# Turning the raw input once: norms applied behind four projections instead of before them, in a two-block transformer kernel

## The chip, the cores and the metric

One core of one Trainium2 chip runs the whole program. The metric is the device time of one execution in microseconds, as the median of several runs. The engines are TensorE (PE, with its weight loads PEld), VectorE (DVE), ScalarE (ACT), GpSimd (POOL) and SyncE (SP, which here issues most of the transfers).

## The reference

Two blocks over 512 tokens of 1024 features, with 16 meta tokens in front (528 tokens in all). Only the start of the first block is touched by the change: the root-mean-square norm and the projections that use it. `w_in` is 1024 x 7168.

```python
def _rms(x, w, eps=1e-6):
    xf = x.astype(jnp.float32)
    y = xf * lax.rsqrt(jnp.mean(xf * xf, axis=-1, keepdims=True) + eps)
    return (y * w.astype(jnp.float32)).astype(x.dtype)
...
        n = _rms(h, norm_mix_w[l])
        z = n @ w_in[l]
        q, k, v, glu, g_att, g_conv = jnp.split(z, splits, axis=-1)
...
        o = _diff_attention(q, k, v, lam, cid)
        y_att = (_rms(o, subln_w[l]) * (1.0 - lambda_init)).reshape(b, lp, ATT_V).astype(h.dtype)
        u = glu[..., :CONV_CH] * jax.nn.sigmoid(glu[..., CONV_CH:])
        u = _causal_dwconv(u, conv_dw_w[l], conv_dw_b[l])
        u = jax.nn.silu(_layernorm(u, conv_ln_w[l], conv_ln_b[l]))
        y_conv = u @ w_conv_out[l]
        m = jax.nn.sigmoid(g_att) * y_att + jax.nn.sigmoid(g_conv) * y_conv
        h = h + m @ w_out[l]
```

The norm's inverse root is one number per token, so a projection of the input times the norm's weight, multiplied per token afterwards, is the same projection. After this come a feed-forward with a short convolution, a second block with three mixers, and its feed-forward.

## The kernel before

Activations lie by feature: 128 features on the partitions, tokens in the free direction, so a projection of 128 output columns is eight k tiles (`step`), each with three products: every fp32 operand is split into a high and a low part of type fp32r (h + l is the value), and high x high, high x low and low x high are added in PSUM. The 528 tokens go as two column segments, so a step is six matmuls of 256 to 264 columns. A weight chunk of 1024 x 128 is loaded by SP into one of three `raw` tiles, ACT makes its high part `wh`, DVE its low part `wl` (`weights`).

The program is written by a planner: `Build` keeps an estimate of PE's time and of DVE's and ACT's, and emits the main stream of projections while side tasks (generators that yield the time until their next step) are put between them; each engine then runs its instructions in the order of emission. All vector and scalar calls are recorded at line 158, all products at line 314, all transposes at line 320. PSUM has two tiles `mm` for the main stream and two tiles `at` for side tasks (`at_get`, `at_put`).

`load_x` loads the tokens as five row tiles `xt` (four of 128, one of 16). `prepare` squares and sums each tile on ACT, takes inverse roots in two groups, scales the rows on DVE into `xs`, and `parts` turns `xs` by 128 x 128 transposes on PE (five for each of eight feature tiles), multiplies by the norm's weight `wmix` and splits the result into the eight operands `xn`, which all projections of the block use. The unscaled input is needed by feature as well, for the residual `res`: feature tiles 0 to 3 are turned while the input loads (16 transposes into the `mm` tiles), the last 16 tokens of these and the feature tiles 4 to 7 by the task `raw`, which runs beside the first projections.

`block1_mix` runs the projections in the order of `units1`: first `glu(0)`, the pair of a convolution input's gate and value halves, k tile by k tile as the operands come, then query, key and value of head 0, the next pair, and so on. ACT evacuates the gate half with a tanh (`e_b`), DVE combines it with the value half (`e_a`); then 33 convolution steps on DVE run in the background (`conv_ops`). Query and key are evacuated by ACT (`e_q`, `e_k`).

## Time and profile before

| | |
|---|---|
| time of the kernel before | 1598.53 us, median of 3 runs (1594.26 to 1602.46) |
| span of the profiled execution | 1592.8 us; the page gives no other time for it |
| PE busy | 1573.0 us, 99% |
| DVE, ACT busy | 1116.7 us, 651.6 us |
| DMA | 134.17 MB, mean 84 GB/s |

The span runs from the first to the last instruction of the profiled execution, and the runs' times are of the whole execution, so the median is compared with the span with some us around it. Lines are those of the kernel before; names are the program's tiles without their numbers: `act` is the pool that holds nearly all activations, `xv` the sums of squares, `rsy` and `rsa` the inverse roots, `u` the convolution's input, `par` the per-channel parameters, `lams` and `lamd` the lambda of the attention.

### The profile page before, as it was taken

Reading aid. Unit: us, or ns where it says so; the run is one execution under the profiler, and the core shown is the slowest. Engines: PE = TensorE matmul, PEld = TensorE weight load, DVE = VectorE, ACT = ScalarE, POOL = GpSimd, SP = SyncE. Lnnn points to the kernel's source line nnn. Section 1 sums busy time; section 2 is a strip of 40 time slices with the busy share of each in tenths; the row PEclk is TensorE's granted clock in tenths of the full one; section 3 lists DMA queues with packets and bytes.
Section 4 is the critical chain, followed back from the end, with each engine's and each line's share of the span. In section 5 each row is a group of like instructions: output and inputs, shape, how many; then the busy total and the mean of one; then the engine's idle time right before and its main releaser. Section 6 shows DMA issues by size and latency. Waiting matters only on the chain.

```text
span 1592.8 us, 25470 instructions
## 1 busy us (share of the span) xinstructions
PE 1573.0 (99%) x10347; PEld 1402.3 (88%) x10349; DVE 1116.7 (70%) x2083; ACT 651.6 (41%) x1166; POOL 26.4 (2%) x85
## 2 busy tenths in 40 slices
PE   7999999999999999999999999999999999999998
PEld 6999999999999999999988878787799888888886
DVE  4989898987766567676753457899868877776224
ACT  5343434445453344344432222634466544444112
POOL 3000000000000000000000000000000000000000
PEclk9999999999999999999999999999999999999999
DMA  4312222212213233333323332232044133332221
GB/s 143 94 57 76 67 80 66 67 55 67 67 54 107 80 93 94 93 94 91 88 86 95 94 93 79 79 94 65 3 133 133 41 99 98 94 93 98 101 93 66
DMA packets 233004, 134.17 MB, mean 84 GB/s; under 512 B 6925, under 2 KB 228240, under 8 KB 232888
## 3 DMA queue, kind: packets, MB, share of 16 engines
q1 hardware_dynamic: 231448, 130.35, 27.9%
q8 instruction: 81, 1.33, 0.3%
q0 software_dynamic: 1136, 1.15, 0.2%
q10 hardware_dynamic: 304, 1.05, 0.2%
q14 instruction: 35, 0.29, 0.1%
HBM read 130.44 MB, written 2.10 MB: 83 GB/s over the span
## 4 chain that ended last, share of the span: by engine, by line
PE 97%; DVE 1%; ACT 1%; DMA 0%; issue 0%; DVEq 0%; ACTq 0%; POOLq 0%
PE mm L314 70%; PE at L314 25%; PE at L320 3%; ACT act L158 0%; DVE act L158 0%; DMA act<-in_x_dram 0%; DVE yy L158 0%; ACT ys L158 0%; DVE yc L158 0%; DVE smx L158 0%; DVE wl L158 0%; DVE fx L158 0%; DVE res L158 0%; DVEq L2194 0%; DVE srl L158 0%
## 5 line engine op out<-in xcount | busy, mean ns | idle before, releaser
L314 PE MATMUL mm<-act,wh 128*128 128x256 f32 (+3 forms) x4720 | 908.1, 306 | 1.2 <-ACT act L158 0.5
L314 PEld LDWEIGHTS mm<-act,wh 128*128 128x128 f32 (+1 forms) x4720 | 692.5, 189 | 51.8 <-issue 9.4
L314 PE MATMUL mm<-act,wl 128*128 128x256 f32 (+4 forms) x2360 | 563.0, 303 | 0.0
L158 DVE TENSOR_TENSOR wl<-raw,wh 128x1024 fp32r<-128x1024 f32 (+2 forms) x235 | 284.4, 1211 | 172.3 <-ACT wh L158 169.8
L158 ACT ACTIVATE wh<-raw 128x1024 fp32r<-128x1024 f32 (+2 forms) x235 | 245.8, 1048 | 377.2 <-PE mm L314 195.6
L314 PEld LDWEIGHTS mm<-act,wl 128*128 128x128 f32 (+1 forms) x2360 | 383.1, 189 | 18.1
L158 DVE SCALAR_TENSOR_TENSOR act<-u,par,act 128x514 f32<-128x514 f32 x232 | 160.4, 747 | 0.0
L314 PE MATMUL at<-act,wh 128*128 128x512 f32 x416 | 130.2, 394 | 0.0
L314 PEld LDWEIGHTS at<-act,wh 128*128 128x128 f32 x416 | 78.0, 188 | 18.3
L314 PE MATMUL at<-wh,act 128*128 128x512 f32 x264 | 85.9, 395 | 0.0
L314 PE MATMUL at<-act,act 128*128 128x256 f32 (+8 forms) x468 | 83.8, 328 | 0.0
L314 PE MATMUL mm<-wh,act 128*128 128x256 f32 (+1 forms) x344 | 83.7, 318 | 0.0
L314 PE MATMUL at<-act,wl 128*128 128x512 f32 x208 | 82.0, 394 | 0.0
L158 DVE TENSOR_TENSOR act<-act,act 128x514 f32<-128x514 f32 (+4 forms) x122 | 69.9, 590 | 6.4 <-ACT act L158 5.8
L158 ACT ACTIVATE act<-mm 128x528 f32<-128x528 f32 (+2 forms) x64 | 35.2, 550 | 94.4 <-PE mm L314 91.8
L314 PEld LDWEIGHTS at<-act,act 128*128 128x128 f32 (+1 forms) x468 | 60.7, 189 | 10.1 <-issue 4.0
L158 DVE SCALAR_TENSOR_TENSOR ft<-fx,par,ft 128x512 f32<-128x512 f32 x88 | 65.8, 749 | 1.6
L158 ACT ACTIVATE act<-at 128x128 f32<-128x128 f32 (+4 forms) x88 | 34.7, 413 | 78.5 <-PE at L314 61.9
L158 DVE TENSOR_TENSOR fx<-mm,rB 128x514 f32<-128x514 f32 x44 | 30.5, 694 | 50.2 <-PE mm L314 50.0
L314 PEld LDWEIGHTS mm<-wh,act 128*128 128x128 f32 x344 | 57.8, 189 | 7.1 <-issue 3.2
L158 DVE SCALAR_TENSOR_TENSOR gy<-gx,par,gy 128x512 f32<-128x512 f32 x84 | 62.6, 749 | 1.5
L314 PEld LDWEIGHTS at<-wh,act 128*128 128x128 f32 x264 | 49.6, 188 | 11.4
(288 smaller groups left out, 1470.6 us busy)
## 6 DMA issues: line engine op xcount, KB each, us to landing
raw<-in_w_in_dram SPq DMA_DIRECT2D x82, 512.0 KB, 3.6
raw<-in_w_up_dram SPq DMA_DIRECT2D x44, 512.0 KB, 3.6
raw<-in_ffn_up_dram SPq DMA_DIRECT2D x44, 512.0 KB, 3.7
raw<-in_ffn_down_dram SPq DMA_DIRECT2D x22, 512.0 KB, 3.2
raw<-in_w_out_dram SPq DMA_DIRECT2D x20, 512.0 KB, 3.8
raw<-in_w_down_dram SPq DMA_DIRECT2D x16, 512.0 KB, 3.6
raw<-in_w_conv_out_dram SPq DMA_DIRECT2D x8, 512.0 KB, 3.7
raw<-in_w_down_dram SPq DMA_DIRECT2D x8, 384.0 KB, 3.3
```

What stands on the lines that cost most here:

```text
L158: return f(*a, **k)
L314: self.nc.tensor.matmul(out, lhsT, rhs, start=start, stop=stop)
L320: self.nc.tensor.transpose(out, src, self.ident[p0 : p0 + k, p0 : p0 + k])
```

## The change

The input is turned once, as it is: feature tiles 0 and 1 row tile by row tile while the input loads, into the two `at` tiles, the others in `parts`. From each turned tile come, in this order, its split times the norm's weight (`xr`), and the copy for the residual (`res`, by ACT). The pair `glu(0)` and query and key of head 0 multiply by `xr`, that is by the input without the inverse norms; these are applied when the results leave PSUM, by DVE with `r0`, the inverse norms of all tokens on every partition, which `stats` makes from the squares (now behind the first splits on ACT), a Newton step, five diagonal tiles and five products with ones. The normed operands `xn` of all other projections are made by `norm`, by feature: DVE multiplies `res` by the weight column and `r0`, and the result is split by ACT and DVE. The scaling by token, the second turning and the task `raw` are gone. The diff below leaves out changes of comments; lines that only say "..." stand for what is left out.

```diff
@@ load_x @@
     def load_x(self):
         nc, io, V, S = self.nc, self.io, self.V, self.S
         x, meta = io["x"][0], io["meta_tokens"]
         self.res = [self.resp.tile([P, NT], F32, name=f"res{j}", tag="res") for j in range(KD)]
-        self.xn = [None] * KD
+        self.xn, self.xr = [None] * KD, [None] * KD
         rows = [P, P, P, P, NMETA]
         xt = [self.flat(D) for _ in range(5)]
-        xs = [self.flat(D) for _ in range(5)]
+        junk = self.flat(D)
         v = self.sm(5, "xv")
         V.memset(v, 1.0)
-        at = (1, 2, 3, 4, 0)
@@ -620,108 +620,103 @@
             else:
                 s = t * P - NMETA
                 q.dma_start(xt[t][: rows[t], :], x[s : s + rows[t], :])
-            self.loaded(xt[t], 5.0 + 1.55 * t)
+            self.loaded(xt[t], 6.5 + 1.2 * t)
...
         wmix = self.const.tile([P, 8], F32, name="wmix")
-
-        def turn(src, pt, j):
-            for t in range(5):
-                w = rows[t]
-                self.tr(pt[:, t * P : t * P + w], src[t][:w, j * P : (j + 1) * P])
-
-        def scale(ts, r, g):
-            c = slice(512 * g, 512 * g + 512)
-            for i, t in enumerate(ts):
-                V.tensor_scalar(xs[t][: rows[t], c], xt[t][: rows[t], c], r[: rows[t], i : i + 1], None, op0=MUL)
-
-        def inverse(lo, n):
-            vb = v[:, lo : lo + n]
-            yield self.due(vb)
-            V.tensor_scalar(vb, vb, 1.0 / D, 1e-6, op0=MUL, op1=ADD)
-            return (yield from self.rsqrt_act(vb, n))
-
-        raws = [self.mm_ps(), self.mm_ps()]
-        rawv = lambda j: raws[j // 2][:, (j % 2) * 512 : (j % 2) * 512 + 512]
+        self.r0 = None
+        rB0 = self.slot()[:, 0, :]
+        def turn(t, pt, j):
+            w = rows[t]
+            self.tr(pt[:, t * P : t * P + w], xt[t][:w, j * P : (j + 1) * P])
 
         def square(t):
-            S.activation(xs[t][: rows[t]], xt[t][: rows[t]], AF.Square, accum_out=v[: rows[t], at[t] : at[t] + 1])
+            S.activation(junk[: rows[t]], xt[t][: rows[t]], AF.Square, accum_out=v[: rows[t], t : t + 1])
 
         def prepare():
             S.activation(self.sm(1, "yw"), v[:, 0:1], AF.Sqrt)
-            self.tr(raws[1][:, 0:8], w8[0:8])
-            yield self.due(raws[1])
-            V.tensor_copy(wmix, raws[1][:, 0:8])
-            square(4)
+            i, pt = yield from self.at_get()
+            self.tr(pt[:, 0:8], w8[0:8])
+            yield self.due(pt)
+            V.tensor_copy(wmix, pt[:, 0:8])
+            self.at_put(i)
+            ats = []
+            for _ in range(2):
+                ats.append((yield from self.at_get()))
+            self.wp_max = 1
             for t in range(4):
                 yield self.due(xt[t])
-                square(t)
-                for j in range(4):
-                    self.tr(rawv(j)[:, t * P : (t + 1) * P], xt[t][:, j * P : (j + 1) * P])
+                for j in range(2):
+                    turn(t, ats[j][1], j)
                 if t == 0:
-                    r = yield from inverse(0, 2)
-                    for g in range(2):
-                        scale((4, 0), r, g)
-            r = yield from inverse(2, 3)
-            scale((1, 2, 3), r, 0)
-            self.wp_max = 1
+                    for j in range(2):
+                        turn(4, ats[j][1], j)
+                    square(4)
+                    square(0)
             for p in range(2):
-                self.start(parts(p))
-            yield self.due(raws[0])
-            for j in range(2):
-                S.activation(self.res[j][:, 0:512], rawv(j), AF.Copy)
-            yield self.due(xs[3][:, 0:512])
-            yield 4.0
-            scale((1, 2, 3), r, 1)
-            for j in range(2, 4):
-                S.activation(self.res[j][:, 0:512], rawv(j), AF.Copy)
-
-        def parts(p):
+                self.start(parts(p, *ats[p]))
+            self.start(stats(), 2.0)
+        def parts(p, i, pt):
             for j in range(p, KD, 2):
-                i, pt = yield from self.at_get()
-                yield self.due(*[xs[t][: rows[t], j * P : (j + 1) * P] for t in range(5)])
-                turn(xs, pt, j)
+                if j != p:
+                    i, pt = yield from self.at_get()
+                    for t in range(5):
+                        turn(t, pt, j)
                 yield self.due(pt)
                 n = self.slot(F32R)
                 self.split_scaled(n, pt[:, :NT], wmix[:, j : j + 1], NT)
-                self.xn[j] = n
+                S.activation(self.res[j], pt[:, :NT], AF.Copy)
+                self.xr[j] = n
                 if j == 1:
                     self.wp_max = 3
-                yield self.due(n)
+                yield self.due(n, self.res[j])
                 self.at_put(i)
 
-        def raw():
...
+        def stats():
+            for t in (1, 2, 3):
+                square(t)
+                yield 1.5
+            yield self.due(v)
+            V.tensor_scalar(v, v, 1.0 / D, 1e-6, op0=MUL, op1=ADD)
+            r = yield from self.rsqrt_act(v, 5)
+            yield from self.bcast_cols(r, rows, rB0, True)
+            yield self.due(rB0)
+            self.r0 = rB0
+            tmp = self.slot()
+            for p in range(2):
+                self.start(norm(p, tmp[:, p, :]))
+        def norm(p, t):
+            for j in range(p, KD, 2):
+                while self.xr[j] is None:
+                    yield 0.2
+                yield self.due(self.res[j])
+                V.scalar_tensor_tensor(t, self.res[j], wmix[:, j : j + 1], rB0, op0=MUL, op1=MUL)
+                yield self.due(t)
+                n = self.slot(F32R)
+                self.split_sb(n, t, NT)
+                self.xn[j] = n
+                yield 0.5
 
         self.feed = [0.0, self.weights()]
         self.start(prepare())
-        self.until(lambda: self.xn[0] is not None)
-        return raw
-
-    def one(self, segs, acts, evac):
+        self.until(lambda: self.xr[0] is not None)
+    def one(self, segs, acts, evac, have=None):
         pt = self.mm_ps()
         lo = segs[0][0]
         n = sum(s[1] for s in segs)
-        self.units([[(pt[:, o : o + m], m, c) for o, m, c in segs]], acts, evac=lambda u: evac(pt[:, lo : lo + n]))
+        self.units([[(pt[:, o : o + m], m, c) for o, m, c in segs]], acts, have=have,
+                   evac=lambda u: evac(pt[:, lo : lo + n]))
@@ block1_mix @@
-            self.start(raw(), 4.0)
             self.start(params(), 14.0)
...
@@ -1080,7 +1074,12 @@
             def glu(s):
                 def e_b(p):
                     hold["tb"] = self.slot()
-                    S.activation(hold["tb"][:, 0, :NT], p, AF.Tanh, scale=0.5)
+                    tb = hold["tb"][:, 0, :NT]
+                    if s == 0:
+                        self.until(lambda: self.r0 is not None)
+                        V.tensor_tensor(tb, p, self.r0, op=MUL)
+                        p = tb
+                    S.activation(tb, p, AF.Tanh, scale=0.5)
 
                 def e_a(p):
                     while len(self.bg) > CK + 2:
@@ -1088,6 +1087,8 @@
                     u = tp.tile([P, CK - 1 + NT], F32, name=self.nm("u"), tag="u")
                     nc.gpsimd.memset(u[:, : CK - 1], 0.0)
                     V.scalar_tensor_tensor(u[:, CK - 1 :], hold["tb"][:, 0, :NT], 1.0, p, op0=ADD, op1=MUL)
+                    if s == 0:
+                        V.tensor_tensor(u[:, CK - 1 :], u[:, CK - 1 :], self.r0, op=MUL)
                     if s % 2 == 0:
                         cv[s // 2] = self.slot()
                     self.until(lambda: "params" in state)
@@ -1101,9 +1102,9 @@
                             if 0 <= kk < 8:
                                 if kk == 0:
                                     ws.append(self.w_take())
-                                self.until(lambda: self.xn[kk] is not None)
+                                self.until(lambda: self.xr[kk] is not None)
                                 self.step([(pts[u][:, o : o + m], m, c) for o, m, c in SEG_ALL], ws[u],
-                                          self.xn[kk], kk, kk == 0, kk == 7)
+                                          self.xr[kk], kk, kk == 0, kk == 7)
                     self.wp_out -= 2
                     e_b(pts[0][:, 248:776])
                     e_a(pts[1][:, 248:776])
@@ -1118,10 +1119,16 @@
                     if h % 2 == 0:
                         ya[h // 2] = self.slot()
                     hold["qk"] = self.slot()
-                    S.activation(hold["qk"][:, 0, :NQ], p, AF.Copy)
+                    if h == 0:
+                        V.tensor_tensor(hold["qk"][:, 0, :NQ], p, self.r0[:, Q0:], op=MUL)
+                    else:
+                        S.activation(hold["qk"][:, 0, :NQ], p, AF.Copy)
 
                 def e_k(p):
-                    S.activation(hold["qk"][:, 1, :], p, AF.Copy)
+                    if h == 0:
+                        V.tensor_tensor(hold["qk"][:, 1, :], p, self.r0, op=MUL)
+                    else:
+                        S.activation(hold["qk"][:, 1, :], p, AF.Copy)
 
                 def e_v(p):
                     hold["vs"] = self.slot()
@@ -1131,7 +1138,9 @@
                     S.activation(hold["vs"][:, 1, :NQ], p, AF.Tanh, scale=0.5)
                     atts.append(self.attention(tp, h, hold["qk"], hold["vs"], (sx, v16, th16, w8, yav(h), state)))
 
-                self.one(SEG_ALL if i in (1, 2) else SEG_Q, self.xn, (e_q, e_k, e_v, e_g)[i])
+                acts = self.xr if h == 0 and i < 2 else self.xn
+                self.one(SEG_ALL if i in (1, 2) else SEG_Q, acts, (e_q, e_k, e_v, e_g)[i],
+                         have=lambda k: acts[k] is not None)
@@ tile_hybrid_kernel @@
-    raw = b.load_x()
-    b.block1_mix(raw)
+    b.load_x()
+    b.block1_mix()
```

## Rows read from the trace of the kernel before

**Rows 1.** The page's first part: each engine's busy time, its share of the span and its instructions.

```profile
PE 1573.0 (99%) x10347; PEld 1402.3 (88%) x10349; DVE 1116.7 (70%) x2083; ACT 651.6 (41%) x1166; POOL 26.4 (2%) x85
```

**Rows 2.** Who PE waited for over the whole span, longest first: us in total, times, longest.

```profile
PE mm L320 <- DMA act<-in_x_dram: 5.3, 2, 4.3
...
PE at L320 <- ACT e L158: 1.2, 2, 1.1
```

**Rows 3.** Busy time in windows of 5 us: stretch, length, then busy us and instructions of PE, PEld (its weight loads), DVE, ACT, POOL, the granted clock, DMA share and GB/s.

```profile
10.00:15.00 5.00, 2.24 (x10) 1.84 (x10) 3.81 (x15) 4.77 (x10) 4.75 (x8) 1.00 0.98 294
...
20.00:25.00 5.00, 4.68 (x29) 3.77 (x28) 3.31 (x5) 2.56 (x4) 0.00 (x0) 1.00 0.39 113
...
25.00:30.00 5.00, 5.00 (x38) 4.48 (x37) 2.49 (x4) 2.11 (x3) 0.00 (x0) 1.00 0.37 108
...
30.00:35.00 5.00, 5.00 (x41) 4.63 (x40) 1.99 (x5) 2.60 (x7) 0.00 (x0) 1.00 0.00 0
...
35.00:40.00 5.00, 5.00 (x40) 4.52 (x38) 1.53 (x7) 2.55 (x4) 0.00 (x0) 1.00 0.00 0
```

**Rows 4.** Timeline of PE, merged where a form repeats: start us, us, engine, line, operation, out<-in, count, and in brackets the idle time before it with what ended it. `mm` are the projections' PSUM tiles, `at` those of the side tasks.

```profile
10.13 1.97 PE L320 MATMUL mm<-ident,act 128*128 128x128 f32 x8 [1.07 <-DMA act<-in_x_dram]
...
17.58 1.25 PE L314 MATMUL mm<-act,wh 128*128 128x264 f32 x4
...
20.39 2.03 PE L320 MATMUL at<-ident,act 128*128 128x128 f32 x10
...
33.45 0.65 PE L314 MATMUL mm<-act,wh 128*128 128x264 f32 x4
...
34.18 0.66 PE L314 MATMUL mm<-act,wh 128*128 128x264 f32 x4
...
38.79 0.64 PE L314 MATMUL mm<-act,wh 128*128 128x256 f32 x4
```

**Rows 5.** The DMA instructions of line 622 (input tiles 1 to 3) and of line 526 (weights) in the first 2.3 us: durations of the issue, first and last start, and the time from issue to landing where the trace matches it.

```profile
L622 ACTq DMA_DIRECT2D act<-in_x_dram x2: 365/404/443, 1.4 to 1.8; - x2
...
DMA to landing us min/median/max: 8.7/8.7/8.7
...
L526 SPq DMA_DIRECT2D raw<-in_w_in_dram x1: 428/428/428, 2.1 to 2.1; - x1
...
DMA to landing us min/median/max: 9.5/9.5/9.5
```

**Rows 6.** Groups of instructions, each shape apart, of the first 45 us or of DVE over the span: line, engine, operation, out<-in, shapes, count | busy us, mean ns of one | idle time before them.

```profile
L158 ACT ACTIVATE act<-at,wmix 128x528 fp32r<-128x528 f32 x8 | 5.6, 701 | 7.6 <-PE at L320 7.6
...
L158 DVE SCALAR_TENSOR_TENSOR act<-at,wmix,act 128x528 fp32r<-128x528 f32 x8 | 6.1, 768 | 5.9 <-ACT act L158 5.9
...
L158 DVE TENSOR_TENSOR wl<-raw,wh 128x1024 fp32r<-128x1024 f32 x5 | 6.1, 1217 | 0.0
...
L158 DVE TENSOR_SCALAR act<-act,rsy 128x512 f32<-128x512 f32 x8 | 3.5, 476 | 0.0
...
L158 DVE TENSOR_TENSOR fx<-mm,rB 128x514 f32<-128x514 f32 x44 | 30.5, 694 | 50.2 <-PE mm L314 50.0
```

**Rows 7.** Timelines of ACT and DVE in the opening (start us, us).

```profile
13.07 0.17 DVE L158 TENSOR_SCALAR xv<-xv 128x3 f32<-128x3 f32 x1 [0.64 <-ACT act L158]
...
18.29 1.05 ACT L158 ACTIVATE wh<-raw 128x1024 fp32r<-128x1024 f32 x1
...
36.80 0.60 ACT L158 ACTIVATE res<-at 128x528 f32<-128x528 f32 x1
...
37.29 0.62 ACT L158 ACTIVATE act<-mm 128x528 f32<-128x528 f32 x1
```

**Rows 8.** PE and its weight loads (PEld) around the sets of transposes and the small products of the opening.

```profile
26.00 0.14 PEld L320 LDWEIGHTS at<-ident,act 128*128 128x128 f32 x1
...
26.80 0.54 PEld L314 LDWEIGHTS mm<-act,wh 128*128 128x128 f32 x4
...
31.54 0.41 PE L320 MATMUL at<-ident,act 16*128 16x16 f32 x4
```

**Rows 9.** A later broadcast of inverse norms, on DVE (diagonal tiles) and PE (the products).

```profile
408.56 1.00 DVE L158 TENSOR_SCALAR act<-ident,rsy 128x128 f32<-128x128 f32 x5
...
410.96 1.37 PE L314 MATMUL at<-act,ones 128*128 128x128 f32 x10
```

**Rows 10.** PE's raw transposes behind the first pair, the first and the last of three sets of five.

```profile
39.51 0.76 PE L320 MATMUL at<-ident,act 128*128 128x128 f32 x5
...
47.85 0.76 PE L320 MATMUL at<-ident,act 128*128 128x128 f32 x5
```

**Rows 11.** DVE later: the first and the last of six windows of 50 us (columns as in rows 3), the convolution's steps (durations in ns min/median/max, first and last start) and the first evacuation of the product behind it.

```profile
50.00:100.00 50.00, 50.00 (x403) 47.46 (x402) 45.74 (x79) 17.07 (x40) 0.12 (x1) 1.00 0.29 85
...
300.00:350.00 50.00, 50.00 (x391) 46.20 (x390) 44.23 (x92) 20.37 (x53) 0.00 (x0) 1.00 0.24 71
...
L158 DVE SCALAR_TENSOR_TENSOR act<-u,par,act x232: 735/747/757, 40.7 to 374.1; 128x514 f32<-128x514 f32 x116
...
474.87 0.69 DVE L158 SCALAR_TENSOR_TENSOR act<-act,mm 128x514 f32<-128x514 f32 x1 [6.77 <-PE mm L314]
```

**Rows 12.** ACT at its second table load.

```profile
32.42 1.28 ACT L158 ACT_TABLE_LOAD   x1
...
33.72 0.20 ACT L158 ACTIVATE lams<-lams 1x2 f32<-1x2 f32 x1
```

16 lines of the change are left out of this document (1 added, 15 removed).

## The prediction

> **What bounds the kernel now.** I read the page first [rows 1]: TensorE (PE) is busy 1573.0 of the span's 1592.8 us, VectorE (DVE) 1116.7, ScalarE (ACT) 651.6. Next the waits of PE over the whole span [rows 2]: beyond the first 25 us there is not 2 us of waiting left, so nearly all of PE's idle time is the opening, and after it a microsecond is worth a microsecond only if it is a microsecond of PE's own work. So the change has two places to act: the start of the first product, and the number of instructions on PE. Then the windows of 5 us [rows 3]: PE is full from 25 us on and nearly so from 20, ACT is nearly full only from 10 to 15, and DVE has a hole from 20 to 40 us, where it is busy 9.3 of 20 us. In the timelines the first product of the first projection pair (call the pair u0) starts at 17.58 us, and the first product of the query projection that follows it (128x256) at 38.79 [rows 4]. Between these lies all that the change does to the pair.
>
> **The start.** Before, the first product waits for a chain: last input tile, its square on ACT, three inverse roots, the scaling on DVE, five transposes, a split. After, it waits for the last tile, two transposes, a split and one weight tile. The last x tile was issued at 1.8 us and landed 8.7 us later, 10.5; the first weight tile was issued at 2.1 and landed after 9.5, 11.6 [rows 5]. The loads keep their order, so these times stay. PE gets to tile 2 at 10.13 [rows 4], and cold transposes follow each other at 0.21 us (ten in 2.03 [rows 4]); the fourth part of feature tile 0 is thus done at about 11.05. From there ACT, in the order in which the program's planner would issue the work (followed by hand through the code; only the order is taken from it): split 0, copy 0, split 1, copy 1, weight 0, square 1, split 2, copy 2, weight 1, split 3, copy 3, square 2, and so on. A copy takes 0.60, but the instruction behind it starts after 0.49 (36.80 and 37.29 [rows 7]); a split with a scale column takes 0.70 [rows 6], so by the same overlap 0.58 start to start. Weight 0 therefore begins at 11.06 + 0.58 + 0.49 + 0.58 + 0.49 = 13.2 and ends at 14.26 (1.05, as at 18.29 [rows 7]). PE has meanwhile to turn feature tiles 2 and 3, which are issued ahead of the first product and wait for the two PSUM tiles: free at 12.6 and 13.7, about 1.05 us each, so PE is through at 14.75. The two meet. I take a first product at 14.8 us, **-2.8 us**. Lower bound 12.7 (weight 0 straight behind split 0), upper 17.6 (the ACT queue eats the gain).
>
> **The pair.** From 17.58 to 38.79 the kernel before needs 21.2 us. Of this the change takes out: the small transposes of the last 16 tokens, 0.41 [rows 8]; one set of five raw transposes, 0.80 (from the first weight load of a set to that of the products behind it, 26.00 to 26.80 [rows 8]); and the sets of feature tiles 2 and 3, 2.03 [rows 4], which now lie before the first product and are already in the 14.8. It adds the broadcast of the inverse norms: ten fp32 records of 128x128 in 1.37 [rows 9]. Net -1.87. The other sets (tiles 4 to 7) stay where they were. What remains is the slack of the opening. 96 products at the warm pace of 0.73 for a step of six (33.45 to 34.18 [rows 4]) make 11.7, the sets of the stretch 3.2 + 2.03 + 0.80 + 0.41; together 18.1, so 3.1 us are cold pace, waits and a few small products. Four products took 1.25 at 17.58 and 0.65 at 33.45 [rows 4]: the granted clock reads 1.00 in all windows [rows 3], yet the pace of the opening (264 columns in about 0.21 us, as a cold transpose step of ten in 2.03) is that of 1.2 GHz. I leave these 3.1 as they are: PE's unbroken work starts some two us earlier and so may its warm pace, but ACT is the tighter engine now. Its work until tile 7 is split is eight splits, eight copies, three squares and three weights (a square of 1024 columns taken like a weight tile, 0.94 start to start), 4.6 + 3.9 + 2.8 + 2.8 = 14.1 us from 11.06, hence 25.2; PE by my sum would need tile 7 at about 31. So ACT is covered, with some 5 us to spare; where the PSUM tiles come back late it is not. Bounds of this slack: 1.1 (two steps at the cold pace, 1.3 against 0.73) and 7.0 (six tiles each late by 0.65, one ACT pass).
>
> The pair would then end 21.2 - 1.9 = 19.3 us after 14.8, at 34.1, against 38.79: **-4.7**.
>
> **After the pair.** Three more raw sets disappear from the stretch of the next two projections (the first at 39.51, the last at 47.85 [rows 10]), 0.80 each with their change-over: **-2.4**. These are pure PE work on a full PE, the surest term.
>
> **What comes in.** The first four evacuations change engine or grow: the gate half of the pair is multiplied on DVE before its tanh, the value half gets one more DVE pass, query and key of head 0 go from ACT to DVE; about 0.69 each (the same form with a broadcast operand, 0.694 [rows 6]). The new wait is at the first: this DVE instruction waits for the broadcast norm (ACT's last square at about 22, six small DVE and ACT steps of about 0.2 as at 13.07 [rows 7], five diagonal tiles in 1.0 [rows 9], the product, a copy: about 27) and for the gate half's product. Behind it on DVE stand the value half, the weight splits and the normed input; the query's first product waits for its PSUM tile. Before, ACT did this at 37.29, more than a microsecond before PE needed the tile [rows 7]. DVE will be full of the normed input just then. I price the stall at **+0.9**: nothing if DVE is free when the gate half is done, 2.2 if a weight split (1.22) and an input step (0.77) [rows 6] stand ahead of it.
>
> DVE's added work: eight products of input, column and norm at 0.77, eight differences at 0.69 as well, four passes at 0.69, five diagonals in 1.0, less ten scalings at 0.48 [rows 6]: 6.2 + 5.5 + 2.8 + 1.0 - 4.8 = +10.7 us. It goes into the hole of 10.7 us between 20 and 40 [rows 3], but only the part after the norm is known, 27 us. The rest must be absorbed later: in the six windows of 50 us from 50 to 350 DVE is busy 44 to 46 us each [rows 11], and the last convolution step is done at 374 [rows 11] while the product that needs the convolution's output has its first result taken at 474.87, where DVE itself waited 6.77 us for PE [rows 11]. So I cost it at nothing. The normed tiles are first needed by the value projection, two projections behind the pair (eight steps of 0.73 each [rows 4], so 5.8 us), at about 46; eight tiles at 1.5 to 2.2 us from 27 are done by 45, each needed only at its own step. ACT's own extra (eight splits of the normed input) falls after 27 us, where it is half idle.
>
> **Sum.** -4.7 - 2.4 + 0.9 = **-6.2 us**, about 1586.6 for the profiled execution's span of 1592.8. The median of the runs, 1598.53, lies 5.7 above that span; the same difference on the median gives **1592.3**. Measured runs of this kernel spread by 0.25% about their median, so changes under 0.5% (8 us) can hardly be told from none.
>
> **Rivals.**
> - *ACT paces the opening.* Each feature tile now needs two ACT passes and a DVE pass before its PSUM tile returns. For it: ACT full from 10 to 15 us [rows 3]. Against: 5 us of spare by the sum above. With the slack at its bound of 7.0 the pair loses 3.9, and the time is 1596.2.
> - *Nothing stalls.* The weight goes ahead of the copies (start 12.7), the first evacuation finds DVE free: -2.1 - 0.9 more, 1589.3. Against: the copies are issued together with their split.
> - *Square root and exponential change places.* In the timeline the exponential of lambda brings a table load of 1.28 us, and the next ACT instruction starts 20 ns behind it [rows 12]. It will come at about 23 us, as will the square root of the norms. If it comes first, ACT loads two tables more, 2 x 1.3 = 2.6 us while the norm is awaited; if all of it reaches PE, 1594.9. For it: the two are within a microsecond of each other in the order; against: the norm has some 6 us to spare. The Trainium skill (ScalarE: Activation LUTs, "Table sets: the hidden batching unit") says that exp and sqrt lie in different sets, and under "What ACT_TABLE_LOAD costs" that every change of set takes 2.66 us with its drain; by that figure, an estimate, this case would cost 5.3 us and give 1597.6. The trace agrees on the load (1.28) and shows no drain behind it.
> - *The other side: DVE becomes the bound.* If the gaps of 4 to 6 us in each 50 are not usable, since they lie between dependent steps, the 10.7 us are paid at the weight splits, which stand in the same queue and which PE needs for every projection. PE's lead of 7.1 is then lost and the convolution stretch ends 10.7 later: 1598.5 + 10.7 = 1609.2. It decides from the point where DVE is behind by more than the two weight tiles in reserve, some 11 us.
>
> **How the numbers follow.** My forecast 0.50, by itself 1589.5 to 1595.5; ACT paces 0.21; nothing stalls 0.18; tables 0.05; DVE bound 0.06. The limit of 0.5% lies at 1590.5: most of "nothing stalls" and a quarter of the forecast is below it, 0.16 + 0.13 = 0.29. Slower by over 0.5% is only the last rival, 0.06. Range: from 1587 ("nothing stalls" with the opening's slack at 1.1 as well is 1587.3) to 1598 (ACT paces and the first stall at 2.2: 1597.5); it leaves out the DVE case and some of the edges.
>
> **What would show it.** First product of the pair at 14 to 15.5 us; the query's first product (128x256) at 33 to 35.5; 40 transposes fewer; no raw transposes after 35 us; ten fp32 records of the broadcast at 25 to 30; DVE busy over 8 of 10 us from 27 to 40; a wait of PE on DVE of about 1 us at the query; and all that follows shifted by one constant. Wrong if the shift grows or shrinks after 60 us (then DVE or the changed order decides), or if PE shows waits on ACT between 15 and 30 us of over 3 us.

## The result, and the profile after

The changed kernel takes 1605.93 us (median; 1601.32 to 1610.05), the kernel before in the same sessions 1595.2: a ratio of 1.0060 (95% interval 1.0048 to 1.0072), 0.6% slower, where 1592.3 was forecast. The times of one kernel spread with the mean clock that its execution was granted (the kernel before 1594 us at 0.999 to 1602 at 0.995, the changed kernel 1601.32 at 0.997 to 1610.05 at 0.990), so a ratio, which counts all runs, can differ from that of the medians. The profiled execution of the changed kernel, 1608.2 us of span, was the longest of its runs: besides what follows it has a stretch at 1166 to 1177 us at half of TensorE's clock, which all but two of the traces below lack and which is left out of the account. The 10 us of the two medians are found without it:

| time of | before | after | later by |
|---|---|---|---|
| first product of the pair | 17.58 | 16.86 | -0.7 |
| first product of the query | 38.79 | 42.29 | +3.5 |
| last value half of the gated pairs on DVE | 305.3 | 306.2 | +0.9 |
| last evacuation of the convolution's output product | 511.34 | 521.00 | +9.7 |
| first mask product of the second block on DVE | 1085.5 | 1095.8 | +10.3 |

So there are two places: the opening (+3.5 where -3.8 was forecast), and the hand-over from the convolution to its output product, between 306 and 521 us (+8.8 where nothing was forecast). In between the raw sets that are gone give their 2.4 back, as forecast (3.5 to 0.9). The 574 us from the fourth to the fifth row of the table took 571.7 to 575.4 us in the fourteen traces of this case, so that a difference of 1 or 2 us there says nothing of a kernel.

The page's first part of the kernel after, which answers [rows 1]: 28 records fewer on PE (40 transposes less, ten products of the broadcast more, less what the trace misses), and DVE 9.5 us more; forecast was 10.7.

```profile
PE 1581.3 (98%) x10319; PEld 1408.3 (88%) x10319; DVE 1126.2 (70%) x2093; ACT 655.2 (41%) x1168; POOL 25.7 (2%) x85
```

Who PE waited for in the kernel after, answering [rows 2] (us in total, times, longest). New are three waits: for DVE at a projection (one of 3.3), for ACT's copies at the transposes, and for the low part of a weight tile.

```profile
PE at L320 <- DMA act<-in_x_dram: 6.0, 2, 4.5
PE mm L314 <- DVE act L158: 3.6, 2, 3.3
PE at L320 <- ACT res L158: 3.0, 3, 2.0
PE mm L314 <- DVE wl L158: 2.8, 1, 2.8
```

**The opening.** ACT in the kernel after (timeline, as [rows 7]). Each copy into the residual (`res`) stands idle for 0.83 us, released by DVE, where 0.49 from one start to the next had been counted; a split and its copy take 2.04 (11.37 to 13.41), not 1.07.

```profile
11.37 0.70 ACT L158 ACTIVATE act<-at,wmix 128x528 fp32r<-128x528 f32 x1 [1.39 <-PE at L320]
12.90 0.61 ACT L158 ACTIVATE res<-at 128x528 f32<-128x528 f32 x1 [0.83 <-DVE act L158]
13.41 0.69 ACT L158 ACTIVATE act<-at,wmix 128x528 fp32r<-128x528 f32 x1
14.94 0.61 ACT L158 ACTIVATE res<-at 128x528 f32<-128x528 f32 x1 [0.83 <-DVE act L158]
15.44 1.05 ACT L158 ACTIVATE wh<-raw 128x1024 fp32r<-128x1024 f32 x1
...
21.50 1.05 ACT L158 ACTIVATE wh<-raw 128x1024 fp32r<-128x1024 f32 x1
```

DVE in the same kernel (timeline):

```profile
12.10 0.77 DVE L158 SCALAR_TENSOR_TENSOR act<-at,wmix,act 128x528 fp32r<-128x528 f32 x1 [8.58 <-ACT act L158]
...
24.20 0.77 DVE L158 SCALAR_TENSOR_TENSOR act<-at,wmix,act 128x528 fp32r<-128x528 f32 x1 [3.25 <-ACT act L158]
24.89 1.22 DVE L158 TENSOR_TENSOR wl<-raw,wh 128x1024 fp32r<-128x1024 f32 x1
```

DVE's low part of the same PSUM tile was emitted ahead of the copy, and the copy waits for it: the two reads of the tile come one after the other (0.77 us of DVE, 12.10 to 12.87, then the copy at 12.90). The Trainium skill (PSUM — Partial Sum Buffer, "PSUM bank collisions raise a hardware error") says that reads of one bank by ScalarE and VectorE collide as well and are to be kept apart by a semaphore; that it is so kept here the rows show, what a collision would do no run does. The second weight tile (21.50, done at 22.55) is late by that. Its low part is later still: on DVE it stands behind the low part of feature tile 4, whose split ACT begins only at 23.48, behind a square, so that DVE idles for 3.25 us with the weight at hand and takes it up at 24.89. PE stops. PE in the kernel after (timeline, as [rows 4]):

```profile
16.86 1.25 PE L314 MATMUL mm<-act,wh 128*128 128x264 f32 x4
...
26.16 0.78 PE L314 MATMUL mm<-act,wl 128*128 128x264 f32 x2 [2.82 <-DVE wl L158]
...
38.02 1.37 PE L314 MATMUL at<-act,ones 128*128 128x128 f32 x10
...
42.29 0.72 PE L314 MATMUL mm<-act,wh 128*128 128x256 f32 x4 [0.30 <-DVE act L158]
```

Behind the wait of 2.82 us the granted clock falls to 1.2 GHz, half of full speed. Windows of the kernel after (columns as in [rows 3]; the last-but-two column is the granted clock): 0.62 and 0.69 of full speed from 25 to 35, where before it was 1.00, and again around 435 and from 475 to 480.

```profile
25.00:30.00 5.00, 3.84 (x15) 3.11 (x16) 3.10 (x3) 4.16 (x7) 0.00 (x0) 0.62 0.35 105
30.00:35.00 5.00, 5.00 (x33) 5.00 (x32) 2.14 (x6) 2.47 (x5) 0.00 (x0) 0.69 0.39 108
430.00:435.00 5.00, 5.00 (x33) 3.73 (x33) 3.40 (x21) 1.05 (x2) 0.00 (x0) 0.74 0.36 107
435.00:440.00 5.00, 5.00 (x25) 3.67 (x24) 2.67 (x6) 2.53 (x7) 0.00 (x0) 0.58 0.01 3
475.00:480.00 5.00, 5.00 (x25) 5.00 (x25) 3.51 (x6) 1.84 (x3) 0.00 (x0) 0.50 0.01 3
```

**The hand-over.** The convolution's steps in the kernel after, first and last start, against 40.7 to 374.1 in [rows 11]: 19.4 and 19.5 later, so what DVE was behind at the start it was still behind at the end.

```profile
L158 DVE SCALAR_TENSOR_TENSOR act<-u,par,act x232: 735/748/756, 60.1 to 393.6; 128x514 f32<-128x514 f32 x116
```

DVE's and PE's timelines of the kernel after at the convolution's output product. The layer norm of the convolution is not done when the last head's inverse norm comes up (`ssv` to `sc`: fifteen steps of some 0.2 us, and a sixteenth of 0.69). They stand ahead of the norm's next low part (`fp32r`, 473.43); PE has nothing else to do, waits 3.26 us for it, and goes on at half pace.

```profile
469.78 0.16 DVE L158 TENSOR_TENSOR ssv<-rl 128x4 f32<-128x4 f32 x1
...
472.62 0.16 DVE L158 TENSOR_TENSOR sc<-rsy,rl 128x4 f32<-128x4 f32 x1
472.82 0.69 DVE L158 TENSOR_TENSOR act<-act,sc 128x512 f32<-128x512 f32 x1
473.43 1.29 DVE L158 TENSOR_TENSOR act<-act,act 128x514 fp32r<-128x514 f32 x2
...
474.17 0.79 PE L314 MATMUL mm<-act,wh 128*128 128x256 f32 x2 [3.26 <-DVE act L158]
```

In the kernel before, all of the norm's low parts were begun by 466.20 and the chain came behind the first evacuation at 474.87 [rows 11], at 475.47:

```profile
475.47 0.16 DVE L158 TENSOR_TENSOR ssv<-rl 128x4 f32<-128x4 f32 x1
```

Up to the first evacuation of the product the stretch from 306 us on is 9.5 us longer than before (485.31 against 474.87, less the 0.9). Three things lie in it: the wait of 3.26, the 7 us at half pace behind it (474 to 481), and 7 us at half pace at 432 to 439, with no wait near; at half pace each of the two costs some 3.4.

### The profile page after: what moved, and what is told of

The parts are those of the page before. It is cut to its first block, busy times and chain, and to the rows that moved or that the text cites. A ratio compares the mean times of both kernels' runs of the same rounds, so it can differ in the third digit from the quotient of the medians.

```text
span 1608.2 us, 25432 instructions
## 1 busy us (share of the span) xinstructions
PE 1581.3 (98%) x10319; PEld 1408.3 (88%) x10319; DVE 1126.2 (70%) x2093; ACT 655.2 (41%) x1168; POOL 25.7 (2%) x85
## 3 DMA queue, kind: packets, MB, share of 16 engines
q8 instruction: 81, 1.33, 0.3%
q0 software_dynamic: 1136, 1.15, 0.2%
## 4 chain that ended last, share of the span: by engine, by line
PE 96%; DVE 1%; ACT 1%; DMA 1%; issue 0%; SPq 0%; DVEq 0%; ACTq 0%
PE mm L314 69%; PE at L314 25%; PE at L320 2%; DVE act L158 1%; ACT act L158 1%; DMA act<-in_x_dram 1%; DVE yy L158 0%; ACT wh L158 0%; DVE wl L158 0%; ACT ys L158 0%; DVE yc L158 0%; ACT res L158 0%; ACT e L158 0%; DVE rsa L158 0%; DVE fx L158 0%
## 5 line engine op out<-in xcount | busy, mean ns | idle before, releaser
L158 DVE TENSOR_TENSOR act<-act,act 128x514 f32<-128x514 f32 (+5 forms) x130 | 75.3, 597 | 5.2 <-ACT act L158 4.5
L158 ACT ACTIVATE act<-mm 128x514 f32<-128x514 f32 (+2 forms) x61 | 33.3, 546 | 101.4 <-PE mm L314 101.4
L158 ACT ACTIVATE act<-at 128x128 f32<-128x128 f32 (+7 forms) x89 | 35.3, 416 | 76.1 <-PE at L314 58.0
L158 ACT ACTIVATE act<-act 128x128 f32<-128x128 f32 (+10 forms) x95 | 51.2, 554 | 23.6 <-DVE act L158 18.6
```

What stands on the lines that cost most here:

```text
L158: return f(*a, **k)
```

## The experiments

All are ratios to the kernel before in the same session; an interval is 95%. What a ratio makes of 1595 us stands behind it.

**The order of the copies alone.** The same instructions; the copy into the residual is emitted ahead of DVE's low part.

```diff
-                self.split_scaled(n, pt[:, :NT], wmix[:, j : j + 1], NT)
+                h, w = n[:, 0, :NT], wmix[:, j : j + 1]
+                S.activation(h, pt[:, :NT], AF.Copy, scale=w)
                 S.activation(self.res[j], pt[:, :NT], AF.Copy)
+                V.scalar_tensor_tensor(n[:, 1, :NT], pt[:, :NT], w, h.bitcast(F32), op0=MUL, op1=SUB)
```

> The changed kernel with one order turned: in each feature tile ACT's copy for the residual is issued before DVE's low part, not after it; same instructions. Theory A (the copy waits 0.83 us for DVE's reading of the same PSUM tile, eight times, so ACT is late with the second weight tile and PE waits and then falls to half pace): ACT's waits for DVE in the opening go, the wait of PE for the weight's low part at 23 us (2.8 us) goes or is under 1 us, the granted clock stays 1.00 from 20 to 40 us, the query's first product comes at 36 to 38 instead of 42.3, and the time is 5 to 8 us under the changed kernel's (about 1599). Rival (the opening is set by the amount of ACT's work, not by the wait): the query at 41 or later, the time within 2 us of the changed kernel's. Theory B (the late convolution costs on its own): the first convolution step comes some 5 us earlier than 59, and a wait of PE for DVE of 0 to 3 us is left between 460 and 480.

Measured 1592.24 us, 0.9984 (0.9973 to 0.9994), -2.6 us; the changed kernel stands at +9.6, so the order alone is worth 12, where 5 to 8 were expected. ACT and DVE of this kernel (timeline):

```profile
11.25 0.70 ACT L158 ACTIVATE act<-at,wmix 128x528 fp32r<-128x528 f32 x1 [1.47 <-PE at L320]
11.85 0.60 ACT L158 ACTIVATE res<-at 128x528 f32<-128x528 f32 x1
12.34 0.70 ACT L158 ACTIVATE act<-at,wmix 128x528 fp32r<-128x528 f32 x1
12.92 0.62 ACT L158 ACTIVATE res<-at 128x528 f32<-128x528 f32 x1
13.41 1.08 ACT L158 ACTIVATE wh<-raw 128x1024 fp32r<-128x1024 f32 x1
...
12.48 0.77 DVE L158 SCALAR_TENSOR_TENSOR act<-at,wmix,act 128x528 fp32r<-128x528 f32 x1 [8.96 <-ACT res L158]
```

The idle 0.83 is gone and the steps have the lengths of the forecast (0.60 and 0.49); now DVE's low part waits for the copy. The first weight starts at 13.41 (forecast 13.2), the first product at 15.82, the query at 35.94; of the wait for the second weight's low part 1.15 us are left, and the clock is 1.00 throughout 25 to 35 us. That settles the opening: 6.4 us. The hand-over still shows its wait, with 4 us at half pace behind it (466 to 470):

```profile
464.75 0.51 PE L314 MATMUL mm<-act,wh 128*128 128x256 f32 x2 [3.27 <-DVE act L158]
...
475.01 0.69 DVE L158 SCALAR_TENSOR_TENSOR act<-act,mm 128x514 f32<-128x514 f32 x1 [5.32 <-PE mm L314]
```

The first evacuation there is 10.3 us earlier than in the changed kernel. What that is beyond the 6.4 lies in the half pace: this trace has none at 432 to 439 us, and less behind the wait.

**No normed input.** The order as in the changed kernel; every projection uses the un-normed parts, so the making of the normed input is left out, 11.7 us of DVE.

```diff
-                V.scalar_tensor_tensor(t, self.res[j], wmix[:, j : j + 1], rB0, op0=MUL, op1=MUL)
-                yield self.due(t)
-                n = self.slot(F32R)
-                self.split_sb(n, t, NT)
-                self.xn[j] = n
+                self.xn[j] = self.xr[j]
```

> The changed kernel without the normed input: the sixteen DVE and eight ACT instructions that make it are left out, and all projections use the input without its inverse norms (so the result is not the reference's). Theory B (DVE's 11 us for it start only at 40 us, push the first convolution step from 40 to 59 and the whole convolution 20 us back, and PE then waits for its output at 471 and falls to half pace): the first convolution step at about 45, the last at about 380, no wait of PE for DVE between 460 and 490, and a time 6 to 9 us under the changed kernel's (about 1598); the opening up to 42 us is as in the changed kernel. Rival (the wait at 471 has another cause, or DVE makes the delay good anyway): the wait stays, the time within 2 us.

Measured 1593.35, 0.9979 (0.9964 to 0.9995), -3.3 us, so some 13 below the changed kernel, where 6 to 9 were expected. The opening is as late as in the changed kernel (query at 42.22, half pace at 26 to 34), but the convolution's last step comes at 378.4 and there is no wait of PE at the hand-over. So the late work on DVE is what is paid at that wait. The half pace at 432 to 439 us is missing here too, which the theory did not foresee.

**Squares at each tile's arrival.** The order of the copies mended, and the squares of tiles 1 to 3 moved ahead of the splits.

```diff
                 if t == 0:
                     ...
                     square(4)
-                    square(0)
+                square(t)
```

> The copy before the low part as in the first kernel, and the squares on ACT as soon as each input tile has landed, ahead of the first splits. Theory A with B: the inverse norms are broadcast some 8 us earlier than in the changed kernel, though the first product starts about 1.5 us later than in the first kernel; the query's first product at 36 to 39; part of the normed input is made before the pair ends, the first convolution step at 48 to 52; PE's wait at 471 gone; 1594 to 1598. Rival (the squares ahead only delay the first product): 2 us slower than the first kernel.

Measured 1600.22, 1.0027 (1.0012 to 1.0042), +4.3 us: the theory's side of this fell, and the loss against the order alone is 7 to 8 us, not the 2 of the rival. The three squares of 1.06 us delay the splits (the first product at 17.91, not 15.82), the query comes at 37.88, and the norm that is known earlier (broadcast at 29.71) buys nothing. These 2 us are what the squares cost; most of the rest is half pace, at 427 to 433 us, where the order alone has none, and at 468 to 479 around a wait of 2.87 on DVE.

**The kernel before with 20 us of idle steps on DVE.** 27 steps of the convolution's kind, into a tile that nobody reads, ahead of the first convolution.

```diff
+                    if s == 0:
+                        z = self.slot()[:, 0, :NQ]
+                        self.bg.append(lambda: V.tensor_scalar(z, u[:, Q0 : Q0 + NQ], self.col("conv_dw_w", 0), None, op0=MUL))
+                        for _ in range(26):
+                            self.bg.append(lambda: V.scalar_tensor_tensor(z, u[:, Q0 : Q0 + NQ], self.col("conv_dw_w", 0), z, op0=MUL, op1=ADD))
```

> The kernel before with 27 more DVE steps (20 us, as long as a convolution step each, into a spare tile) ahead of the first convolution: nothing else is changed. Theory B: the delay of 20 us is not made good, the last convolution step comes at about 393 instead of 374, PE waits 2 to 5 us for DVE at 460 to 480 and may run at half pace behind it; the time is 4 to 9 us over the kernel before. Rival (DVE's free 4 to 6 us in each 50 absorb 20 us by 374, as the prediction costed it): the last step at 374 to 380, no new wait, the time within 1.5 us of the kernel before.

Measured 1610.48, 1.0101 (1.0078 to 1.0124), +16 us, where 4 to 9 were expected: DVE's delay is not absorbed in the 430 us up to the hand-over. It grew instead: the planner places other work by its estimate of DVE, the last value half comes at 314.4 (305.3 before), and the convolution ends 35 us later than before, not 20. So this run shows the place and the sign, and not the price of 20 us. The waits of PE name the convolution's output product, and the clock is at half from 469 to 490 us:

```profile
L158 DVE SCALAR_TENSOR_TENSOR act<-u,par,act x258: 735/749/756, 40.8 to 409.2; 128x514 f32<-128x514 f32 x129
...
PE mm L314 <- DVE act L158: 6.4, 6, 3.3
```

**Both causes out.** The order mended and no normed input.

> The changed kernel with both suspected causes taken out at once: the copies into the residual emitted ahead of VectorE's low parts (same instructions, other order), and the normed input left out (every projection takes the un-normed parts, so a part of the computation is missing and VectorE has 11.7 us less to do). Theory (two separate losses, one in the opening worth some 6 us, one at the hand-over of the convolution worth some 10): the opening as in the kernel with the order alone (query's first product at 36.0 +-0.5), the last convolution step before 378, no wait of TensorE on VectorE at 460 to 490 us, first evacuation behind the convolution at 468 to 471, and the whole at 1586 to 1589. Rival (one cause seen twice: once the convolution is in time, or once the opening is early, the other gives nothing more): the better of the two alone, 1592 to 1594.

Measured 1589.76, 0.9963 (0.9951 to 0.9976), -5.9 us; the query at 36.01, the convolution's last step at 372.2, no wait on DVE at the hand-over. Better than either alone, a little above the theory's 1586 to 1589. The two are not additive: singly 12 and 13 us below the changed kernel, together 15.5. In the traces the last evacuation of the convolution's product is 10.3 and 9.5 us earlier singly and 15.4 together; the 4.3 that are in both are of the size of the half pace at 432 to 439 us (3.4), which none of the three traces has.

**The products of the normed input on GpSimd.**

```diff
-                V.scalar_tensor_tensor(t, self.res[j], wmix[:, j : j + 1], rB0, op0=MUL, op1=MUL)
+                self.G.tensor_tensor(t, self.res[j], rB0, op=MUL)
                 yield self.due(t)
                 n = self.slot(F32R)
-                self.split_sb(n, t, NT)
+                self.split_scaled(n, t, wmix[:, j : j + 1], NT)
```

(on top of the mended order; `self.G` records GpSimd in the planner as the other lanes are recorded.)

> The copies ahead of the low parts, and the eight products of the residual with the broadcast norm given to GpSimd, which is idle there; the column weight moves into the split (ScalarE's copy with a scale, VectorE's low part). All of the computation is there. VectorE has eight products fewer (8 x 0.77 = 6.2 us). Theory (the backlog of VectorE is paid at the hand-over to the convolution's output): the convolution's last step some 6 us earlier than with the order alone (387 to about 381), the wait of 3.3 us on VectorE behind it gone or under 1.5, and the whole at 1588 to 1591. Rival (GpSimd is slow at this and makes the normed tiles late, or slows VectorE while it runs): a wait of TensorE for the normed tiles between 42 and 60 us, convolution no earlier, 1592 to 1597.

Measured 1596.66, 1.0008 (0.9988 to 1.0029): the rival was right, no gain, and the convolution ends at 391.3, later than with the order alone (387.2). PE now waits twice for the normed tiles, and the clock is at half from 55 to 62 us; the wait at the hand-over (3.26) is still there. The first of the two waits, and groups of DVE from 30 to 60 us in this kernel:

```profile
54.42 0.51 PE L320 MATMUL mm<-act,wh 128*128 128x264 f32 x2 [1.86 <-DVE act L158]
...
L158 DVE SCALAR_TENSOR_TENSOR act<-act,wmix,act 128x528 fp32r<-128x528 f32 x8 | 9.5, 1196 | 0.5 <-ACT act L158 0.5
L158 DVE TENSOR_TENSOR wl<-raw,wh 128x1024 fp32r<-128x1024 f32 x4 | 7.0, 1779 | 0.0
...
L158 DVE TENSOR_TENSOR act<-mm,act 128x528 f32<-128x528 f32 (+1 forms) x3 | 2.1, 694 | 0.3 <-ACT act L158 0.3
```

and with the order alone, in the same stretch:

```profile
L158 DVE TENSOR_TENSOR wl<-raw,wh 128x1024 fp32r<-128x1024 f32 x5 | 6.1, 1218 | 0.0
L158 DVE SCALAR_TENSOR_TENSOR act<-res,wmix,act 128x528 f32<-128x528 f32 x8 | 5.9, 762 | 0.3 <-ACT act L158 0.3
...
L158 DVE TENSOR_TENSOR act<-mm,act 128x528 f32<-128x528 f32 (+1 forms) x3 | 2.1, 695 | 0.0
```

While GpSimd runs its products (1.74 us each), DVE's steps with two operands in SBUF take half as long again (1196 against 762, 1779 against 1218), those with one operand in PSUM as long as ever (694 against 695). What was taken from DVE came back as slower steps: eight low parts of 1196 ns, which were plain differences of 702 with the order alone, and four weight splits longer by 561 make 6.2 us, as much as the eight products that went (an estimate from these rows). The Trainium skill (SBUF — State Buffer, "SBUF: two separate sides") says that a DVE step with two SBUF inputs and a GpSimd step that reads SBUF lock each other out of one pair of ports; the rows agree.

**The meta tokens' attention 12 us later.** For the half pace at 432 to 439: there the layer norm's ten products of one column and sixteen products of two rows lie within 5 us in the changed kernel, which in the kernel before lay apart.

```diff
                 while "heads" not in state:
                     yield 0.3
+                yield 12.0
                 yield from self.first_queries((sx, v16, th16, w8, None), xa, yav)
```

> The changed kernel with the attention of the last two meta tokens started 12 us later, so that its small products no longer lie beside the layer norm's sums of one column; nothing else is moved. Theory (the low clock at 432 to 439 us comes from the two groups of small products lying together, as they did not before): full clock through 427 to 445, the first evacuation behind the convolution some 3 us earlier than 485.3, unless the wait on VectorE takes it back (then it is longer by as much); the whole at 1602 to 1606. Rival (the low clock there comes from something else): the same windows at the low clock, or the same loss some 12 us later, 1606 +-1.5.

Measured 1602.19, 1.0037 (1.0023 to 1.0052), 3.7 us below the changed kernel. The clock is 1.00 from 430 to 440, as the theory had it, but a shorter dip comes at 449 to 453, right behind the sixteen products (446.62), which now have the ten 21 us ahead of them. That is the loss "some 12 us later" of the rival. And PE, which is earlier at the hand-over, waits there for longer (2.77 us for DVE and 1.30 for ACT, with half pace behind): the first evacuation comes at 484.44, 0.9 and not 3 us earlier. The time lies in the theory's range all the same, and its mechanism fell: lying together is not needed for the drop. It isn't enough for it either. With the order alone the two groups lie as close as in the changed kernel, and the clock stays at 1.00. The sixteen products in the changed kernel, then with the order alone:

```profile
431.32 2.56 PE L314 MATMUL at<-act,xaT 16*2 16x128 f32 x16
...
424.93 1.90 PE L314 MATMUL at<-act,xaT 16*2 16x128 f32 x16
```

Where the gain of 3.7 comes from is not shown: at the first mask product of the second block this trace is 2.3 us ahead of the changed kernel's, at the convolution's last evacuation 1.0.

**Two taps of each convolution tile on ACT.** 16 passes of 0.51 us taken from DVE, in three kernels: the mended order, the kernel before, the changed kernel.

```diff
-            lambda: V.tensor_scalar(a, u[:, 0:NQ], w(0), self.col("conv_dw_b", j), op0=MUL, op1=ADD),
-            lambda: V.tensor_scalar(b, u[:, 1 : 1 + NQ], w(1), None, op0=MUL),
+            lambda: self.S.activation(a, u[:, 0:NQ], AF.Identity, bias=self.col("conv_dw_b", j), scale=w(0)),
+            lambda: self.S.activation(b, u[:, 1 : 1 + NQ], AF.Copy, scale=w(1)),
```

> The order of the copies mended, and the first two taps of each of the eight convolution tiles (16 passes of 0.51 us on VectorE) given to ScalarE, which is busy 20 of 50 us there: 8.2 us taken from VectorE in the stretch where it has no room. All of the computation is there. Theory (VectorE's added work is not absorbed but carried to the hand-over of the convolution at 420 to 485 us): the last convolution step at about 379 instead of 387, no wait of TensorE over 1 us on VectorE at 460 to 475, first evacuation behind the convolution near 470, the whole some 3 us below the order alone, 1588 to 1590.5. Rival (the steps between are bound by something else, the backlog only looks like the cause): convolution's end and the wait of 3.3 us as with the order alone, 1592 +-1.

> The kernel before with the same 16 passes given to ScalarE. The control: there TensorE does not wait for the convolution, so the relief of VectorE should buy nothing. Theory: the convolution's last step some 8 us earlier than 374, the whole unchanged within 1.5 us. Rival (the relief helps by itself, whatever the change does): 3 us or more below before.

> The changed kernel as it is, with the same 16 passes given to ScalarE. Theory: the opening as before the relief (query at 42.2), the convolution's last step at about 385, the wait at the convolution's first product under 1.5 us, the whole 4 to 9 us below the changed kernel: 1596 to 1601. Rival: no more than 2 us below it, 1603 to 1606.

Measured 1597.43, 1599.46 and 1600.49 us, as ratios 0.9990 (0.9972 to 1.0007), 1.0014 (1.0001 to 1.0027) and 1.0016 (1.0001 to 1.0032). The first is the rival's outcome: the last step at 385.9 (387.2 without), the wait of 3.26 still there. Its median stands above the rival's 1592; its trace has a stretch at half pace from 1153 us on, like that of the changed kernel at 1166. Who DVE waited for from 50 to 400 us there:

```profile
DVE wl L158 <- ACT wh L158: 9.9, 11, 1.8
DVE act L158 <- ACT act L158: 8.3, 8, 2.2
```

and with the order alone:

```profile
DVE wl L158 <- ACT wh L158: 4.7, 10, 1.5
...
DVE act L158 <- ACT act L158: 2.7, 6, 0.8
```

The 8.2 us came back as 10.8 us of waiting for ACT, which now has the taps ahead of the weights' high parts. The control missed too: in the kernel before the convolution ended 11.5 us earlier (362.6) and the time was not better but 2.2 us worse (4.3 by the medians), with a wait of PE on DVE of 1.84 and half pace at 479 to 483:

```profile
473.88 0.16 DVE L158 TENSOR_TENSOR ssv<-ssv,ss 128x4 f32<-128x4 f32 x1 [4.38 <-ACT act L158]
...
477.28 0.68 DVE L158 SCALAR_TENSOR_TENSOR act<-act,mm 128x514 f32<-128x514 f32 x1
...
478.01 0.74 PE L314 MATMUL mm<-act,wh 128*128 128x256 f32 x4 [1.84 <-DVE act L158]
```

Here the layer norm was done in time, but the last head's chain came up ahead of the first evacuation (477.28), which in the kernel before it follows, and DVE stood in it for 4.38 us waiting for ACT. So it isn't the lateness alone that is paid; what counts is what stands on DVE ahead of the step that PE comes for. In the third kernel the convolution ended at 391.6 (385 expected) and the wait of 3.27 stayed; its first evacuation (481.71) is 3.6 us earlier than the changed kernel's, which is the size of the half pace at 432 to 439; its trace lacks that, although the same small products lie there at the same times.

**The chain of small steps behind the layer norm.** That last reading, tested: the last head's sixteen steps wait in emission until the layer norm's last tile is issued.

```diff
             yield self.due(ss0)
+            while h == 7 and None in state["us"]:
+                yield 0.1
             v = self.sm(4, "ssv")
```

> The order of the copies mended, and besides it one chain of VectorE moved: the sixteen small steps that make the last head's inverse norm (some 3 us, 460.35 to 464.0 in the run with the order alone) are issued behind the last tile of the layer norm and not ahead of it; the same instructions, all of the computation. Theory (the 3.3 us that TensorE waits at the convolution's output are this chain, behind which the late layer norm's low parts stand; the drop to the low clock at 464 to 469 follows from the wait): no wait of TensorE over 1 us between 455 and 475, full clock there, first evacuation behind the convolution at 469.5 to 471.5 instead of 475.0, the whole 3 to 6 us below the order alone: 1586.5 to 1589.5. Rival (the layer norm itself is late, the chain only happens to stand there): a wait of 2 us or more remains at the same place or at a later tile of the same projection, 1591 to 1593.

> The changed kernel as it is, with the same chain moved and nothing else. Theory: the opening and the low clock at 26 to 34 us as in the changed kernel (query at 42.2), but no wait of 3.3 us at 471 to 474 and no low clock behind it, first evacuation behind the convolution at 479 to 481 instead of 485.3, the whole 4 to 7 us below the changed kernel: 1599 to 1602. Rival (the layer norm itself is 10 us late): the wait remains in another place, 1604 to 1606.

With the mended order: 1588.04 us, 0.9961 (0.9945 to 0.9977), -6.2 us, faster than both kernels. In the changed kernel alone: 1596.88 us, 1.0011 (0.9999 to 1.0024), +1.8, so 7.8 below the changed kernel (9.0 by the medians, where 4 to 7 was expected). DVE and PE of the first of the two:

```profile
460.85 1.30 DVE L158 TENSOR_TENSOR act<-act,act 128x514 fp32r<-128x514 f32 x2 [0.47 <-ACT act L158]
...
463.39 0.51 PE L314 MATMUL mm<-act,wh 128*128 128x256 f32 x2 [0.81 <-DVE act L158]
...
465.86 0.16 DVE L158 TENSOR_TENSOR ssv<-rl 128x4 f32<-128x4 f32 x1
...
470.70 0.69 DVE L158 SCALAR_TENSOR_TENSOR act<-act,mm 128x514 f32<-128x514 f32 x1 [1.18 <-PE mm L314]
```

The convolution ends as late as with the order alone (387.2), and yet the wait is 0.81, the clock stays at 1.00, and the first evacuation comes 4.3 us earlier (470.70 against 475.01). The rival, that the layer norm itself is too late, falls. In the changed kernel, whose convolution ends as late as ever (393.7), the wait is 0.81 too, no half pace follows, and the first evacuation comes at 478.71 instead of 485.31.

## Why the prediction was wrong

**Right in size.** The transposes that go (28 records with the ten of the broadcast), the broadcast's 1.37, the three raw sets behind the pair (the shift goes from +3.5 to +0.9, forecast -2.4), DVE's added work (9.5 against 10.7), the stall at the first evacuation (0.30 against 0.9, within its bounds), and no harm from the tables. With both orders mended the kernel gains 6.2 us by its ratio, which is the sum that was forecast, by 6.8 us between the medians. That the figures are equal is in part luck: the opening then gives a little less (first product 15.77, forecast 14.8; query 35.90, forecast 35.0 with its stall), the last evacuation of the convolution's product is 4.8 us earlier than before and not 6.2, and the rest comes in a stretch whose length differs by up to 3.7 us between the traces.

**Wrong: the base.** The 5.7 us between median and span came from a median of three runs (1594.26, 1598.53, 1602.46). Twelve runs give 1595.2, 2.4 above the span; the same sum is then 1589.0.

**Wrong: the start and ACT's cover.** The first failed step is "a copy takes 0.60, but the instruction behind it starts after 0.49", taken for all eight copies from a copy in [rows 7] that read a PSUM tile of its own. Here DVE reads the same tile and is emitted ahead. A split with its copy took 2.04 from start to start, not 1.07; over eight tiles that makes ACT's 14.1 us some 21.9, the "5 us to spare" are gone, and "ACT paces the opening" is the case that came, with the slack beyond its upper bound of 7.0: the first product at 16.86, and 25.4 us instead of 20.2 to the query. Part of it is the order on DVE, where a weight that was ready stood behind a feature tile that was not. A microsecond of the start stays wrong with the order mended (15.82 against 14.8): the PSUM tile comes back only with DVE's low part, at 13.25 and not at 12.6, and the ten transposes behind it take 2.59 us, not 2.1. The working followed the order by hand and saw which engine issues what; it didn't ask which semaphore the second reader of a tile gets.

**Wrong: the clock.** It was read as 1.00 and left so. Each wait of 2.8 to 3.3 us on a full PE was followed by 3 to 8 us at 1.2 GHz, and by 10 and 21 where further waits came in between; at half pace 3 to 8 us are some 2 to 4 more, up to as much as the wait again. The bounds of the first stall and of the opening's slack held none of it.

**Wrong: "must be absorbed later", "So I cost it at nothing".** This is the second failed step. The gap between 374 and 474.87 us was read as slack. In it lies the layer norm of the convolution, whose sums start at 405.72 before and 430.12 after, and whose low parts share DVE's queue with the last heads. What is idle on DVE there (5 us in 50) did not take up the delay: it was 19.4 us at the convolution's first step and 19.5 at its last. The norm was known 13 us later than counted (the normed input starts at 40.08, not 27). Half of that came from the opening (33.73 with the mended order); with it the convolution is 13 us late, in the changed kernel 19.5. The rival "DVE becomes the bound" named the side and 1609.2, near by luck: its mechanism did not come, since no weight split held up PE after the opening.

**What decided.** Not the amount of work on DVE, but whose steps stand ahead of whose at the hand-over: sixteen small steps, 3.65 us in all, moved behind the last tiles of the layer norm give back 6.6 us at the first evacuation of the changed kernel, most of what 19 us of delay seemed to cost (some 1.7 of it is the shorter half pace at 433 to 437).

**Open.** What brings the half pace at 432 to 439 us, some 3.4 us of the changed kernel's loss. That the small products lie together is refuted as the cause: in five traces (the order alone, GpSimd, the mended order and the changed kernel with the taps on ACT, the mended order with the chain moved) they lie just as close without it. Where the drop is there (the changed kernel, 433 to 437 with the chain moved in it, 427 to 433 with the squares early, 449 to 453 with the attention later), it comes behind the sixteen products of two rows; in the other ten traces the same sixteen run at 1.00. There is one trace of each kernel, so whether the drop belongs to a kernel or to an execution isn't shown.

## What to carry to other kernels

When a change adds work to an engine that isn't the bound, don't look for its idle time in windows: find the next instruction of the bound that needs that engine's result, and list what stands ahead of it in the queue once the engine is late. Where two engines read one PSUM tile, look at which read is emitted first, since the other gets a wait, and let the engine that is short of time read first. A wait of some 3 us on a full TensorE cost one and a half times to over twice its length here, with the half pace behind it. And a drop of the clock that one trace shows is not yet the kernel's: look for the same instructions in the other traces before explaining it.

## What was not expected of the hardware

- Waits of TensorE of 2.8 to 3.3 us on otherwise full work were followed by 1.2 GHz for 8 us (26 to 34) and 7 us (474 to 481) in the changed kernel and 4 us with the order alone (466 to 470). Single waits of 1.84 (478.01 in the kernel before with the taps on ACT) and 1.86 (54.42 in the kernel with GpSimd) were followed by it too; one of 1.15 at 22.77 was not (order alone). A wait of 1.07 for ACT, which stands in all fourteen traces (1153.88 before, 1164.21 after), was followed by 11 us and more at half pace in three (the changed kernel, both causes out, the mended order with the taps) and by none in eleven.
- TensorE's clock also fell without any wait, with PE busy in all 5.00 us, behind sixteen products of two rows (432 to 439); this in four traces of fourteen, while in the other ten it stayed at 1.00 behind the same products.
- GpSimd's product of two 128x528 tiles took 1.33 us in its shortest rows and 1.74 on average, and slowed DVE's weight split beside it from 1.22 to as much as 2.35 us.
